# Second summands of weight halves added one half product sooner on VectorE, with their loads, in a two-layer mixer

## The chip, the cores and the metric

The kernel runs on one core of a Trainium2 chip. The metric is the device time of one execution in microseconds (us), median of the runs; lower is better. Engines are named as the profile names them: PE (TensorE matmul), DVE (VectorE), ACT (ScalarE), POOL (GpSimd), SP (SyncE, which here only issues loads).

## The reference

Two post-norm layers over a residual stream of 512 rows by 2048 columns. Each layer projects the stream once, runs three groups of heads, gates them, projects back and normalises:

```
h = einsum('bsd,dn->bsn', x, w_in)             # 2048 -> q, k, v, gates of 16 heads, index q/k/w
y_fox = fox_attention(...) * silu(fg)          # 6 heads, forget gate
y_dsa = dsa_attention(rope(dq), rope(dk), dv, q_idx, k_idx, w_idx) * silu(dg)   # 6 heads, top 128 of 512 keys
y_mem = memory_attention(mq, k_mem, v_mem) * silu(mg)                           # 4 heads, 256 memory rows
y = concat(y_fox, y_dsa, y_mem) @ w_out
x = layer_norm(ALPHA * x + y, ln_gain, ln_bias)
```

All is float32, and the result has to be that of float32 products. The top 128 keys of each query row come from an index score that all heads share.

## The kernel before

**Products.** A float32 product is made of three matmuls: each operand is split into a high part and the remainder (`split`: ACT writes `whi`, the high part; DVE writes `wlo`, the remainder, raw minus `whi`), and `product` sums hi\*hi, hi\*lo and lo\*hi. The large projections are also cut into 2x2 blocks and multiplied with seven products in place of eight (`PRODUCTS`: P1, P7, Q4, P2, Q6, Q5, Q3), some of whose right sides are sums of weight blocks.

**The stream.** `stream()` fixes a list of chunks of weights for both layers: memory values and keys, the index projection, then the *values* stage (`vs` chunks, all projections of values, gates and head inputs, six column pairs), the *heads* stage (Q5 and Q3 of the same projections, while the attention heads run) and the *out* stage. A chunk is 128 x 2048 floats and is used in two halves of 512 KB, h = 0 and 1. The main loop goes over halves, n = 2i + h. In the values stage a half is 12 matmuls of 128 x 512 columns on PE. For each column pair the chunks come in the order P1 0, P7 0, P1 1, P7 1, P2 0, Q6 0, Q6 1, P2 1, Q4 0, Q4 1 (the digit is the block of 1024 rows of weights), then one or two head chunks.

**Where right sides come from.** Most chunks are loaded as they are ("wall"). Sums for P7 of pair 0, for Q5 and for the out stage are made in DRAM by POOL, with accumulating transfers (tile `sum`), and then loaded. Q6 and Q4 are made on chip from raw halves that are done with (`make_w`, `raw<-raw,raw` on DVE). P7 of pairs 1 to 5 ("pair") is a sum of two weight blocks: `load_w` loads the first block's half into `raw` (SP, L373) and the second block's half as two tiles `other` of 128 x 512 (SP, L379), and `pair_w` adds the two on DVE, in two instructions `raw<-raw,other` of 128 x 512.

**What sets the order.** Each engine executes its instructions in the order in which the program emits them, and waits at each until its operands are there. In step n of the main loop the program emits, in this order: the loads of a chunk two ahead (`load_w`), `split_w(n + 3)` (ACT `whi`, DVE `wlo`, then `make_w` where that half gives a raw away), `pair_w(n + 4)`, the matmuls of half n, and, between them (`advance`, `tick`), pieces of the other work: the top-128 search (on DVE: `m<-acc` MAX, then `acc<-m,acc` MATCH_REPLACE), residual rows, copies of finished values. Raw halves live in seven buffers (`raws`), and a load waits for the last reader of the buffer's tenant before; `whi` and `wlo` have four buffers each. `other` tiles come from a shared pool of 69 slots, which values on their way to DRAM use as well. SP issues all loads of weights, of residual rows (`z<-x`, `row`) and of head inputs, in program order.

**Names for halves below.** In one column pair, m and m+1 are the halves of P7 0, m+2 and m+3 those of P1 1, m+4 and m+5 those of P7 1; m-2 and m-1 are those of P1 0. So m, m+1, m+4 and m+5 need a second summand.

Of the kernel before, what the change touches and what calls it, by code (L numbers as in the profile page):

```python
# [35 lines left out]
SCALE = HD ** -0.5  # L36
SOON, LATER, URGENT, DUE = 1.5, 4.0, 5.0, 10.0
SLOTS = 69
PACE = 2
R_ATTEND, R_QK, R_LOAD, R_MEM = 4, 5, 4, 8  # L40

# [216 lines left out]
def kernel(  # L258
# [13 lines left out]
    clock = Clock()  # L272
    nc = Engines(tc.nc, clock)
    consts = ctx.enter_context(tc.tile_pool(name="consts", bufs=1))
    raws = ctx.enter_context(tc.tile_pool(name="raws", bufs=7))
    whl = ctx.enter_context(tc.tile_pool(name="whl", bufs=4))
    slots = ctx.enter_context(tc.tile_pool(name="slots", bufs=SLOTS))
    tiny = ctx.enter_context(tc.tile_pool(name="tiny", bufs=3))
# [6 lines left out]
    def uid(name):  # L285
        count[0] += 1
        return f"{name}_{count[0]}"
# [43 lines left out]
    chunks = stream()  # L331
    raw, parts = {}, {}
# [46 lines left out]
                        nc.sync.dma_start(t, wall[key[1]][:, e * 512:(e + 1) * 512])  # L379

    others = {}

    def pair_w(n):

        i, h = divmod(n, 2)
        if i < len(chunks) and chunks[i][4][0] == "pair":
            for e in range(2):
                d = raw[i][h][:, e * 512:(e + 1) * 512]
                nc.vector.tensor_tensor(d, d, others.pop((i, 2 * h + e)), op=ALU.add)
# [160 lines left out]
    def block(kind, l, pair, g, step):  # L550
        return wall[where[kind, l, 2 * pair + step[1], 2 * step[0] + g]]

    def add_weights(key, src):
        nc.gpsimd.dma_start(sums[key], src, accum_op=ALU.add, max_dma_last_dim=2 * DM)

    def weight_sums(kind, l, names, pairs, some=(0, 1)):

        for name in names:
            for n in some:
                step = SUM_STEPS[name][n]  # L560
                for pair in pairs:
                    for g in range(2):
                        key = (kind, l, name, pair, g)
                        src = block(kind, l, pair, g, step)
                        pool_waits()
                        if n:
                            add_weights(key, src)
                        else:
                            sums[key] = dram.tile([P, DM], F32, name=uid("sum"))
                            nc.gpsimd.dma_start(sums[key], src, max_dma_last_dim=2 * DM)  # L570
                        yield

    def paced(gen):

        n = 0
        for _ in gen:
            n += 1
            while now[1] in ("kv", "heads"):
                yield 1
            yield {"out": 3, "index": 1 + n % 2}.get(now[1], PACE)  # L580

# [1020 lines left out]
    for i, (kind, l, j, col, _) in enumerate(chunks):  # L1602
        late = last_half(i)
        if kind == "out":
            step = OUT_ORDER.index(j)
            name, pair = j
# [3 lines left out]
            chain, aname, _, targets = PRODUCTS[name]  # L1610
# [9 lines left out]
        elif kind == "vs":  # L1620
            name, pair = j
# [13 lines left out]
        for h in range(2):  # L1635
            n = 2 * i + h
# [1 line left out]
            if n in late_makes:  # L1638
                make_w(late_makes[n])
            if i > 0:  # L1640
                late_half = i > 8 and i + 2 < len(chunks) and chunks[i + 2][4][0] != "pair"
                if late_half:
                    load_w(i + 2, 2, (h,))
                elif h == 0:
                    load_w(i + 2)
            if h == 0 and i > 0:
                if 2 <= i < 6:
                    for k in range(4 * i - 8, 4 * i - 4):
# [8 lines left out]
                splits[n + 3] = flow(split_steps(n + 3), 1e9, clock.at["PE"] + DUE)  # L1657
            else:
                split_w(n + 3)
            pair_w(n + 4)  # L1660
            for k in range(2 * n - 20, 2 * n - 18) if n < 16 else range(12, 16) if n == 16 else ():
                if k >= 0:
                    split_x(k)
# [43 lines left out]
            elif kind == "mk":  # L1707
                for kk in range(8):
                    k = 8 * h + kk
                    m = memT[k // 2]  # L1710
# [13 lines left out]
        if kind == "mk":  # L1724
            t = slot("kmem", F32R)
# [19 lines left out]
        elif kind == "small":  # L1745
# [4 lines left out]
            t = index_rope(ps, 64, 0, nc.vector)  # L1750
# [8 lines left out]
        elif kind == "iq":  # L1759
            t = index_rope(ps, P, P, nc.vector)  # L1760
# [137 lines left out]
```

## Time and profile before

| | |
|---|---|
| time, median of 3 runs (lowest to highest) | 1885.79 us (1884.57 to 1889.16) |
| profiled execution | 1885.75 us, span 1884.0 us |
| PE busy | 1854.5 us, 98% |
| DVE busy | 1606.9 us, 85% |
| ACT busy | 1079.0 us, 57% |
| POOL busy | 404.9 us, 21% |
| mean granted clock of TensorE | 0.997 of full |
| adds of second summands on DVE | 80, median 685 ns each |
| makes on DVE (`raw<-raw,raw`) | 88, median 1225 ns each |
| remainders on DVE (`wlo`) | 497, mean 1217 ns each |

Busy times are sums over one execution. A row of the timeline has its start (us from the span's start), its length, engine, line, operation, written tile, read tiles, shape and, in brackets, the engine's idle time before it with what ended that time. All compute instructions have line L242, a helper that records each of them; so groups are told apart by tile, not by line. A run of equal instructions stands as one row with a count (x2).

### The profile page before, as it was taken

Reading aid. Unit: us, or ns where it says so; the run is one execution under the profiler, and the core shown is the slowest. Engines: PE = TensorE matmul, PEld = TensorE weight load, DVE = VectorE, ACT = ScalarE, POOL = GpSimd, SP = SyncE. Lnnn points to the kernel's source line nnn. Section 1 sums busy time; section 2 is a strip of 40 time slices with the busy share of each in tenths; the row PEclk is TensorE's granted clock in tenths of the full one; section 3 lists DMA queues with packets and bytes.
Section 4 is the critical chain, followed back from the end, with each engine's and each line's share of the span. In section 5 each row is a group of like instructions: output and inputs, shape, how many; then the busy total and the mean of one; then the engine's idle time right before and its main releaser. Section 6 shows DMA issues by size and latency. Waiting matters only on the chain.

```text
span 1884.0 us, 26451 instructions
## 1 busy us (share of the span) xinstructions
PE 1854.5 (98%) x8994; PEld 1574.5 (84%) x8994; DVE 1606.9 (85%) x2565; ACT 1079.0 (57%) x1752; POOL 404.9 (21%) x595
## 2 busy tenths in 40 slices
PE   9999999999999999999999999999999999999997
PEld 8998888887888888888899977877878888888886
DVE  6789889888789987889887997898797898878798
ACT  5776344435347887555476653444354578875553
POOL 0121222122134311330011121221221343113302
PEclk9999999999999999999999999999999999999999
DMA  9885998898999978986598869988989998889866
GB/s 350 294 240 160 302 298 242 303 279 274 253 239 298 241 217 218 268 209 214 174 322 250 228 204 302 329 270 288 284 274 246 247 306 226 222 213 276 237 215 144
DMA packets 232165, 478.40 MB, mean 254 GB/s; under 512 B 76624, under 2 KB 101200, under 8 KB 231772
## 3 DMA queue, kind: packets, MB, share of 16 engines
q1 hardware_dynamic: 177660, 302.58, 49.8%
q0 software_dynamic: 53792, 173.06, 35.7%
q8 instruction: 71, 1.16, 0.2%
q10 hardware_dynamic: 576, 1.05, 0.1%
q14 instruction: 66, 0.54, 0.1%
HBM read 404.24 MB, written 152.07 MB: 295 GB/s over the span
## 4 chain that ended last, share of the span: by engine, by line
PE 70%; DVE 14%; DMA 8%; issue 4%; ACT 3%; SPq 0%; POOL 0%; DVEq 0%; ACTq 0%; POOLq 0%
PE v L242 30%; PE c L242 17%; PE z L242 15%; DVE wlo L242 6%; DMA other<-in_wall_dram 4%; DMA raw<-in_wall_dram 3%; PE po L242 3%; DVE raw L242 2%; PE s L242 2%; DVE acc L242 1%; ACT whi L242 1%; PE ix L242 1%; PE pt L242 1%; DMA v<-vraw 1%; DVE rope L242 1%
## 5 line engine op out<-in xcount | busy, mean ns | idle before, releaser
L242 ACT ACTIVATE whi<-raw 128x1024 fp32r<-128x1024 f32 (+1 forms) x497 | 521.2, 1056 | 473.5 <-PE v L242 190.9
L242 DVE TENSOR_TENSOR wlo<-raw,whi 128x1024 fp32r<-128x1024 f32 (+1 forms) x497 | 601.0, 1217 | 115.8 <-ACT whi L242 113.6
L242 PE MATMUL v<-whi,vxh 128*128 128x512 f32 x768 | 306.3, 399 | 6.8 <-ACT whi L242 3.2
L242 PE MATMUL v<-wlo,vxh 128*128 128x512 f32 x768 | 301.4, 392 | 7.9 <-DVE wlo L242 7.9
L242 PE MATMUL v<-whi,vxl 128*128 128x512 f32 x768 | 300.5, 391 | 0.0
L242 PE MATMUL v<-whi,xh 128*128 128x512 f32 x576 | 224.2, 389 | 0.0
L242 PE MATMUL v<-whi,xl 128*128 128x512 f32 x576 | 224.1, 389 | 0.0
L242 PE MATMUL v<-wlo,xh 128*128 128x512 f32 x576 | 224.1, 389 | 0.0
L242 PE MATMUL c<-xh,whi 128*128 128x512 f32 (+1 forms) x544 | 197.9, 364 | 0.0
L242 PE MATMUL c<-xh,wlo 128*128 128x512 f32 (+1 forms) x544 | 197.8, 364 | 0.0
L242 PE MATMUL c<-xl,whi 128*128 128x512 f32 (+1 forms) x544 | 197.7, 363 | 0.0
L242 POOL TENSOR_TENSOR seen<-mark,mhalf 128x1 f32<-128x1 f32 x88 | 48.3, 549 | 636.3 <-ACT mark L242 447.3
L242 PEld LDWEIGHTS v<-whi,vxh 128*128 128x128 f32 x768 | 144.7, 188 | 40.1 <-ACT whi L242 7.2
L242 PEld LDWEIGHTS v<-wlo,vxh 128*128 128x128 f32 x768 | 144.9, 189 | 39.3 <-DVE wlo L242 12.5
L242 PE MATMUL z<-wlo,yh 128*128 128x512 f32 (+1 forms) x434 | 167.8, 387 | 2.3 <-DVE wlo L242 2.3
L242 PEld LDWEIGHTS v<-whi,vxl 128*128 128x128 f32 x768 | 144.5, 188 | 30.4
L242 PE MATMUL z<-whi,yh 128*128 128x512 f32 (+1 forms) x434 | 168.6, 389 | 0.0
L242 PE MATMUL z<-whi,yl 128*128 128x512 f32 (+1 forms) x434 | 167.7, 387 | 0.0
L242 PEld LDWEIGHTS v<-wlo,xh 128*128 128x128 f32 x576 | 108.1, 188 | 22.6
L242 PEld LDWEIGHTS v<-whi,xh 128*128 128x128 f32 x576 | 108.1, 188 | 22.5
L242 PEld LDWEIGHTS v<-whi,xl 128*128 128x128 f32 x576 | 108.1, 188 | 22.5
L242 PEld LDWEIGHTS c<-xl,whi 128*128 128x128 f32 x544 | 102.1, 188 | 12.2
(209 smaller groups left out, 3459.9 us busy)
## 6 DMA issues: line engine op xcount, KB each, us to landing
raw<-in_wall_dram SPq DMA_DIRECT2D x331, 512.0 KB, 7.3
sum<-in_wall_dram POOLq DMA_DIRECT2D x88, 1024.0 KB, 10.4
raw<-sum SPq DMA_DIRECT2D x72, 512.0 KB, 7.4
v<-vraw POOLq DMA_DIRECT2D x88, 256.0 KB, 8.8
other<-in_wall_dram SPq DMA_DIRECT2D x80, 256.0 KB, 13.7
vt<-halves POOLq DMA_DIRECT2D x56, 256.0 KB, 9.4
vraw<-v SPq DMA_DIRECT2D x56, 256.0 KB, 5.1
grown<-in_wall_dram POOLq DMA_DIRECT2D x48, 256.0 KB, 8.9
```

The costliest lines, as they stand in the source:

```text
L242: return f(*args, **kw)
```

## The change

Three things are changed. `pair_w` is called with n + 5 instead of n + 4, so that the adds of a half's second summand come one split earlier in DVE's order. Loads go through `load_half`, which loads each half once; the halves of a "pair" chunk are loaded one step sooner than before (`soon`), to go with that. And `load_more` issues, in each step after chunk 8, up to two further halves, up to 14 halves ahead, as long as fewer than six of the seven raw buffers are in use, and only sums that POOL finished 20 us before by the planner's clock.

```diff
+RAWS, FAR, SETTLE = 7, 14, 20.0
...
+    loaded, settled = set(range(6)), {}
+
+    def load_half(m):
+        if m not in loaded:
+            loaded.add(m)
+            load_w(m // 2, 2, (m % 2,))
+
+    def raws_used():
+        return len({id(t) for v in raw.values() for t in v if t is not None and not isinstance(t, list)})
+
+    def load_more(n):
+
+        m = n + 4
+        for _ in range(2):
+            while m in loaded or (m < 2 * len(chunks) and chunks[m // 2][4][0] == "grown"):
+                m += 1
+            if m > n + FAR or m >= 2 * len(chunks) or raws_used() >= RAWS - 1:
+                return
+            kind, l, j, _, (how, key) = chunks[m // 2]
+            if kind == "out" and j[0] == "P7" or how == "pair" and len(others) > 2:
+                return
+            if how == "sum" and settled.get(key, 1e9) + SETTLE > clock.at["PE"]:
+                return
+            load_half(m)
...
                         if n:
                             add_weights(key, src)
+                            settled[key] = clock.at["PE"]
...
             if i > 0:
-                late_half = i > 8 and i + 2 < len(chunks) and chunks[i + 2][4][0] != "pair"
-                if late_half:
-                    load_w(i + 2, 2, (h,))
-                elif h == 0:
-                    load_w(i + 2)
+                soon = chunks[min((n + 5) // 2, len(chunks) - 1)][4][0] == "pair" or i <= 8 and h == 0
+                for m in (n + 4, n + 5) if soon else (n + 4,) if i > 8 else ():
+                    load_half(m)
...
-            pair_w(n + 4)
+            pair_w(n + 5)
+            if i > 8:
+                load_more(n)
```

The orders of PE, ACT and POOL stay as they were; DVE's and SP's move. The numbers behind a tile's name are buffers and differ between the two kernels; lines after the new functions shift by one, then by 27.

The first place is DVE at P7 0 of column pair 4 of layer 1. Before (`raw_13188` is half m, `raw_13194` half m+1, `raw_13146` and `raw_13164` the raws of P1 0, halves m-2 and m-1; `m<-acc` and `acc<-m,acc` are the top-128 search):

```order
L242 TENSOR_TENSOR wlo_13201<-raw_13164,whi_13200 128x1024
L242 TENSOR_TENSOR raw_13188<-raw_13188,other_13190 128x512
L242 TENSOR_TENSOR raw_13188<-raw_13188,other_13192 128x512
L242 MAX m_2827_13235<-acc_10251 128x8
L242 MATCH_REPLACE acc_10251<-m_2827_13235,acc_10251 128x512
L242 TENSOR_TENSOR wlo_13243<-raw_13188,whi_13242 128x1024
L242 TENSOR_TENSOR raw_13188<-raw_13188,raw_13146 128x1024
L242 TENSOR_TENSOR raw_13194<-raw_13194,other_13196 128x512
L242 TENSOR_TENSOR raw_13194<-raw_13194,other_13198 128x512
L242 MAX m_2833_13275<-acc_10251 128x8
L242 MATCH_REPLACE acc_10251<-m_2833_13275,acc_10251 128x512
L242 TENSOR_TENSOR wlo_13285<-raw_13194,whi_13284 128x1024
```

The same place in the changed kernel (`raw_13089` is half m, `raw_13118` half m+1, `raw_13038` and `raw_13067` the raws of P1 0; `vraw` are finished values leaving PSUM):

```order
L243 TENSOR_TENSOR raw_13089<-raw_13089,other_13093 128x512
L243 TENSOR_TENSOR vraw_12871<-vraw_12871,v_12800 128x512
L243 TENSOR_TENSOR vraw_12879<-vraw_12879,v_12801 128x512
L243 MAX m_2823_13202<-acc_10261 128x8
L243 MATCH_REPLACE acc_10261<-m_2823_13202,acc_10261 128x512
L243 TENSOR_TENSOR wlo_13207<-raw_13067,whi_13206 128x1024
L243 TENSOR_TENSOR raw_13118<-raw_13118,other_13120 128x512
L243 TENSOR_TENSOR raw_13118<-raw_13118,other_13122 128x512
L243 MAX m_2829_13241<-acc_10261 128x8
L243 MATCH_REPLACE acc_10261<-m_2829_13241,acc_10261 128x512
L243 TENSOR_TENSOR wlo_13249<-raw_13089,whi_13248 128x1024
L243 TENSOR_TENSOR raw_13089<-raw_13089,raw_13038 128x1024
```

The adds of m+1 stood behind `wlo` and the make of m; now they stand ahead of both, and the adds of m ahead of `wlo` of m-1 and of two reads of PSUM.

The second place is DVE at P7 1 of the same pair. Before (`raw_13330` is m+4, `raw_13336` m+5, `raw_13302` m+3):

```order
L242 TENSOR_TENSOR wlo_13343<-raw_13302,whi_13342 128x1024
L242 TENSOR_TENSOR raw_13330<-raw_13330,other_13332 128x512
L242 TENSOR_TENSOR raw_13330<-raw_13330,other_13334 128x512
L242 TENSOR_TENSOR wlo_13361<-raw_13330,whi_13360 128x1024
L242 TENSOR_TENSOR raw_13330<-raw_13330,raw_13282 128x1024
L242 TENSOR_TENSOR raw_13336<-raw_13336,other_13338 128x512
L242 TENSOR_TENSOR raw_13336<-raw_13336,other_13340 128x512
L242 MAX m_2857_13379<-acc_10251 128x8
L242 MATCH_REPLACE acc_10251<-m_2857_13379,acc_10251 128x512
L242 TENSOR_TENSOR wlo_13385<-raw_13336,whi_13384 128x1024
```

and in the changed kernel (`raw_13253` is m+4, `raw_13297` m+5, `raw_13142` and `raw_13168` are m+2 and m+3):

```order
L243 TENSOR_TENSOR wlo_13317<-raw_13142,whi_13316 128x1024
L243 TENSOR_TENSOR raw_13253<-raw_13253,other_13255 128x512
L243 TENSOR_TENSOR raw_13253<-raw_13253,other_13257 128x512
L243 MAX m_2850_13339<-acc_10261 128x8
L243 MATCH_REPLACE acc_10261<-m_2850_13339,acc_10261 128x512
L243 TENSOR_TENSOR wlo_13345<-raw_13168,whi_13344 128x1024
L243 TENSOR_TENSOR raw_13297<-raw_13297,other_13299 128x512
L243 TENSOR_TENSOR raw_13297<-raw_13297,other_13301 128x512
L243 TENSOR_TENSOR wlo_13363<-raw_13253,whi_13362 128x1024
L243 TENSOR_TENSOR raw_13253<-raw_13253,raw_13142 128x1024
L243 MAX m_2858_13381<-acc_10261 128x8
L243 MATCH_REPLACE acc_10261<-m_2858_13381,acc_10261 128x512
```

Between the adds of m+4 and the remainder of m+4 there now stand one search step, the remainder of m+3 and the adds of m+5.

The third place is SP ahead of P7 0 of column pair 2 of layer 1, where loads of residual rows (`z<-x`, `row`) share the queue. Before:

```order
L373 DMA raw_11872<-in_wall_dram 128x1024
L1455 DMA row_11985<-in_gain_dram 128x512
L1455 DMA row_11987<-in_bias_dram 128x512
L1519 DMA z_11989<-x_183 128x512
L373 DMA raw_11994<-in_wall_dram 128x1024
L373 DMA raw_12014<-in_wall_dram 128x1024
L373 DMA raw_12042<-in_wall_dram 128x1024
L373 DMA raw_12060<-in_wall_dram 128x1024
L373 DMA raw_12084<-in_wall_dram 128x1024
L379 DMA other_12086<-in_wall_dram 128x512
L379 DMA other_12088<-in_wall_dram 128x512
```

and in the changed kernel:

```order
L374 DMA raw_11879<-in_wall_dram 128x1024
L374 DMA raw_11902<-in_wall_dram 128x1024
L374 DMA raw_11920<-in_wall_dram 128x1024
L374 DMA raw_11953<-in_wall_dram 128x1024
L374 DMA raw_11975<-in_wall_dram 128x1024
L380 DMA other_11977<-in_wall_dram 128x512
L380 DMA other_11979<-in_wall_dram 128x512
L1482 DMA row_11999<-in_gain_dram 128x512
L1482 DMA row_12001<-in_bias_dram 128x512
L1546 DMA z_12003<-x_183 128x512
```

The raws and the first half's second summand (`raw_12084` before, `raw_11975` now, is half m) stood behind the residual row's loads and now stand ahead of them. At the start of layer 1's values stage and in both heads stages raws move ahead of residual rows and of head inputs in the same way; in layer 0's values stage and in pairs 4 and 5 of layer 1 SP's order of loads of weights and residual rows is as before; in pair 3 of layer 1 three loads of residual rows change places with one or two raws.

More of the change, by code (lines that the diff above doesn't have):

```diff
@@ L274 @@
     consts = ctx.enter_context(tc.tile_pool(name="consts", bufs=1))
-    raws = ctx.enter_context(tc.tile_pool(name="raws", bufs=7))
+    raws = ctx.enter_context(tc.tile_pool(name="raws", bufs=RAWS))
     whl = ctx.enter_context(tc.tile_pool(name="whl", bufs=4))
```

## Prediction, before the changed kernel was run

> **What bounds the kernel now.** The page first: which engine fills the span, and what DVE waits for.
>
> ```profile
> span 1884.0 us, 26451 instructions
> PE 1854.5 (98%) x8994; PEld 1574.5 (84%) x8994; DVE 1606.9 (85%) x2565; ACT 1079.0 (57%) x1752; POOL 404.9 (21%) x595
> ...
> L242 DVE TENSOR_TENSOR wlo<-raw,whi 128x1024 fp32r<-128x1024 f32 (+1 forms) x497 | 601.0, 1217 | 115.8 <-ACT whi L242 113.6
> ...
> other<-in_wall_dram SPq DMA_DIRECT2D x80, 256.0 KB, 13.7
> ```
>
> PE is busy for 1854.5 of 1884.0 us, so only some 30 us can be had from waits at all, start and end among them. The profiled execution took 1885.75 us, 1.75 more than its span and 0.04 less than the median, so a sum against it is a sum against the median. DVE's 113.6 us of waiting for ACT before a remainder look large, and an add next to its own remainder makes part of them: but idle time on DVE counts only where PE runs dry. So the second view is PE's busy time by stretches of the values stage (start to end, length, PE busy, granted clock, share of the DMA engines, GB/s).
>
> ```profile
> 425.00:480.00 55.00, 53.70 (x236) 1.00 0.85 278
> 1083.00:1130.00 47.00, 44.65 (x200) 1.00 0.69 203
> 1130.00:1180.00 50.00, 48.47 (x206) 0.97 0.92 305
> 1180.00:1240.00 60.00, 58.44 (x257) 1.00 0.97 312
> 1300.00:1346.00 46.00, 45.04 (x198) 1.00 0.81 239
> 1346.00:1378.00 32.00, 29.31 (x126) 1.00 0.90 270
> ```
>
> They leave 1.30, 2.35, 1.53, 1.56, 0.96 and 2.69 us idle, 10.4 in all: the ends of P7 in layer 0's pair 4 and layer 1's pairs 1 to 4, and the start of layer 1's values stage. Third, PE's own rows: where it stalls, and for whom.
>
> ```profile
> 1113.21 0.50 PE L242 MATMUL v<-wlo,vxh 128*128 128x512 f32 x1 [1.76 <-DVE wlo L242]
> ...
> 1164.61 0.39 PE L242 MATMUL v<-whi,vxl 128*128 128x512 f32 x1
> 1165.78 0.50 PE L242 MATMUL v<-whi,vxh 128*128 128x512 f32 x1 [0.78 <-ACT whi L242]
> 1167.04 0.59 PE L242 MATMUL v<-wlo,vxh 128*128 128x512 f32 x1 [0.76 <-DVE wlo L242]
> 1167.42 0.63 PE L242 MATMUL v<-whi,vxl 128*128 128x512 f32 x1
> 1167.85 0.63 PE L242 MATMUL v<-whi,vxh 128*128 128x512 f32 x1
> ...
> 1171.27 0.40 PE L242 MATMUL v<-whi,xh 128*128 128x512 f32 x1
> 1171.50 0.40 PE L242 MATMUL v<-wlo,xh 128*128 128x512 f32 x1
> ...
> 1358.55 0.50 PE L242 MATMUL v<-wlo,vxh 128*128 128x512 f32 x1 [0.83 <-DVE wlo L242]
> ...
> 1370.86 0.50 PE L242 MATMUL v<-whi,vxh 128*128 128x512 f32 x1 [0.90 <-ACT whi L242]
> 1372.16 0.50 PE L242 MATMUL v<-wlo,vxh 128*128 128x512 f32 x1 [0.80 <-DVE wlo L242]
> ```
>
> Undisturbed matmuls start 0.23 us apart (1171.27, 1171.50), 12 to a half, so a half lasts 2.72 us (estimate). From 1164.61 to 1165.78 and on to 1167.04 there are 1.17 and 1.26, so the two stalls lose 0.94 and 1.03, 2.0 together, somewhat more than the idle columns say. Behind them matmuls start 0.43 apart (1167.42, 1167.85). There the granted clock is low:
>
> ```profile
> 1164.00:1168.00 4.00, 2.46 (x9) 0.91 0.62 200
> 1168.00:1172.00 4.00, 4.00 (x14) 0.66 0.59 122
> ```
>
> The missing 0.09 and 0.34 of 4 us each are 1.7 us, which stand as busy time. So layer 1's pair 1 costs 3.7, not 2.0. With this, 10.4 + 1.7 and some 1.0 for what the idle columns hide, the values stage holds about 13 us; more the change can't gain there.
>
> Fourth, DVE in the worst pair (layer 1, pair 4), from m to m+5:
>
> ```profile
> 1347.85 1.23 DVE L242 TENSOR_TENSOR raw<-raw,raw 128x1024 f32<-128x1024 f32 x1
> ...
> 1355.28 0.69 DVE L242 TENSOR_TENSOR raw<-raw,other 128x512 f32<-128x512 f32 x1 [2.58 <-DMA other<-in_wall_dram]
> 1355.89 0.69 DVE L242 MAX8 m<-acc 128x8 f32<-128x512 f32 x1
> ...
> 1357.28 1.22 DVE L242 TENSOR_TENSOR wlo<-raw,whi 128x1024 fp32r<-128x1024 f32 x1
> ...
> 1365.89 1.23 DVE L242 TENSOR_TENSOR wlo<-raw,whi 128x1024 fp32r<-128x1024 f32 x1 [1.26 <-ACT whi L242]
> ...
> 1370.89 1.22 DVE L242 TENSOR_TENSOR wlo<-raw,whi 128x1024 fp32r<-128x1024 f32 x1
> ```
>
> Two waits are to be seen. At 1355.28 DVE waits for the second summand of m+1 to land; at 1365.89 it waits 1.26 for ACT's `whi`, because add and remainder of m+4 are neighbours. The tile's own view has the sums (what ended idle time before the adds, and before those that waited for the adds; us, times):
>
> ```profile
>   DMA other<-in_wall_dram: 33.1, 20
> ...
>   ACT whi L242: 107.7, 28
> ```
>
> The neighbours' wait is what the change removes. The landing is older and is the cause here: from 1355.28 to 1370.89 DVE idles only for that 1.26, and PE waits for its last remainder. After a late second summand DVE's work bounds PE.
>
> **The change, part by part.**
>
> *Late pairs whose summands land when they did.* After the last late add, DVE's order before held five remainders, two makes, two double adds and three search steps until m+5 is split; 15.6 us from 1355.28 to 1370.89, the 1.26 idle included. In the new order the remainder of m and its make stand behind that add too, and one more search step: 1.22 + 1.23 + 1.39 (1355.89 to 1357.28) = 3.84, of which starts overlap by some 0.1 each, so 3.6. The idle 1.26 goes, since a search step and another half's work lie between. Net +2.4, say +2.5. From the other side: if DVE runs under a PE that has enough split halves, it costs nothing. Layer 1's pair 4 is behind already (2.69 us idle): +2.5. Layer 0's pair 4 and layer 1's pair 3 have stalls at the end of P7 (1.30 and 0.96 idle): +2 each, as part of it meets what is left of slack. Layer 0's pair 1 shows no stall at P7: +1, between 0 and 2.5. Sum +7.5, bounds 0 and +10.
>
> *The remainder of m now waits for m+1's summand.* In pair 4 it would start at 1357.3, where the one of m+1 stood, and end near 1358.5. On PE m+1 began near 1358.5 after a stall of about 1.1, so m, 2.72 earlier and without that stall, is due near 1354.7: PE would stand some 3.8 us in one place. This is not added: it is the same lateness, moved forward, and the end is still set by DVE's chain.
>
> *Buffers.* The raw of m+5 takes the buffer that the make of m frees:
>
> ```profile
> 1349.14 0.33 SPq L373 DMA_DIRECT2D raw<-in_wall_dram  x1
> ...
> DMA to landing us min/median/max: 14.4/14.4/14.4
> ...
> DMA to landing us min/median/max: 4.7/4.7/4.7
> ```
>
> It was issued at 1349.14, as the make (1347.85 + 1.23) ended, and took 14.4 us among the others; one issued near 427.5 with little around it took 4.7. The make now ends behind the add at 1355.28: + 0.69 + 1.39 + 1.22 + 1.23 = 1359.8, so this load starts 10.7 later. Its add is due about 1368.5: 1359.8 and, in the new order, a search step (1.39), a remainder, a make and a remainder (1.15 each from start to start), the adds of m+4 (1.3), a search step (1.39) and a remainder (1.2). Landing at 1364.5 (4.7) it is hidden; at 1374.2 (14.4), with its second summand some 1.5 behind, the pair loses 7. By then the queue is nearly empty, as the other loads of the pair were issued before, so I take the value near 4.7: +0.4 for each of four late pairs, +1.5; bounds 0 and +28.
>
> *Loads ahead in layer 1.* In pair 2 SP stood still in front of a residual row:
>
> ```profile
> 1180.63 0.33 SPq L1455 DMA_DIRECT2D row<-in_bias_dram  x1
> 1188.64 0.33 SPq L1519 DMA_DIRECT2D z<-x  x1
> 1189.07 3.93 SPq L373 DMA_DIRECT2D raw<-in_wall_dram  x5
> 1196.77 2.28 SPq L379 DMA_DIRECT2D other<-in_wall_dram  x2
> ```
>
> Five raws came 8 us late and then together, and the second summand behind them. With the raws ahead of `row` and `z` that goes, and the second summand leaves about 4 us sooner (half of the 8, as it waits for transfers in flight as well). That covers the +2.5 of the longer chain and the present 1.56: -1.5, between 0 and -2. In pair 1 it leaves sooner in the same way (an estimate from the same rows): the stalls of 2.0 go, and likely the low clock behind them: -3, between 0 and -3.7. At the stage's start:
>
> ```profile
> 1084.72 2.24 ACT L242 ACTIVATE whi<-raw 128x1024 fp32r<-128x1024 f32 x2 [1.55 <-DMA raw<-in_wall_dram]
> ```
>
> ACT waits there for raws that now leave some 10 us sooner; the 2.35 us of the first window hang on this partly, and partly on the operands of the left side: -1.5, between 0 and -2.4.
>
> *Heads and out.* Here raws and sums go ahead of head inputs, which then leave up to some 14 us later (estimate from SP's order and the times before). The tightest of them shows:
>
> ```profile
> POOL bt L242 <- DMA ck<-crow: 21.8, 4, 8.4
> ```
>
> POOL already waits for `ck` up to 8.4 us at four heads while PE goes on with the products; POOL is busy for 21% of the span. I cost this at 0; with that cover gone, +4 (half of the 8.4 once more, in one layer).
>
> Sum: 7.5 + 1.5 - 1.5 - 3 - 1.5 = +3.0, and 1885.75 + 3.0 = 1888.8, rounded to **1889 us**.
>
> **Rivals.** *The neighbours' wait is the bound* (faster). For it: each stall at m+5 is a wait for `whi`, then `wlo`, right behind an add (1165.78, 1370.86), and the change takes just these apart; second summands may also land sooner in every pair. Against it: the chain from 1355.28 has no other slack, and gets longer. Then most of the 13 us go: 1873 to 1878, say 1876.
>
> *The freed buffer decides* (slower). The raw of m+5 leaves 10.7 us later, takes nearer 14.4 than 4.7, and the remainder of m+4, which now stands behind the add of m+5, waits too. It decides from a landing of more than 9 us on. Then four late pairs lose 3 to 7 more than the chain: about 1889 + 12 = 1901. Against it: the emptier queue.
>
> *Head inputs behind the raws* (slower): +4 and the +3, 1893.
>
> *Crowding* (slower). The DMA engines are busy for 0.92 and 0.97 of pairs 1 and 2 of layer 1 (windows above). Raws sent ahead then only change places with the second summands in flight, the three gains fall to their bounds of 0, and 1885.75 + 9.0 is 1895. Against it: the 8 us in which SP issued nothing. The Trainium skill ("DMA: Bandwidth & Descriptors", Issuing engines are not separate DMA queues) speaks for it: transfers of all issuing engines share the same DMA engines and interleave. The shares agree with that.
>
> *The gate* (slower). PE's stall of 3.8 us in the two pairs 4 and a like one in layer 1's pair 3 let the clock fall as at 1167: 1.7 us in each, if PE and not DVE then sets the end: 1889 + 5 = 1894. Against it: behind such a stall DVE is later than PE. By the Trainium skill ("TensorE: Matmul & The Clock Gate", HAM oscillation) an idle gap of more than about 3.4 us closes the gate; this trace differs, since two gaps of about 1 us closed it at 1167 and two like them at 1370 did not.
>
> *Nothing*: the waits move and the work under PE takes up both, 1886.
>
> **How the numbers follow.** What a measurement of this kernel can tell from no change is about 0.3%, 5.7 us: faster is below 1880, slower above 1891.5. The forecast has 0.40 (0.03 faster, 0.27 same, 0.10 slower, its terms as uncertain as their bounds), the neighbours 0.25 (0.22 faster, 0.03 same), the buffer 0.17 (0.15 slower, 0.02 same), heads 0.05 (0.02 slower, 0.03 same), crowding 0.04 (slower), the gate 0.04 (0.03 slower, 0.01 same), nothing 0.05 (same). Faster 0.25, same 0.41, slower 0.34. The range takes in the forecast, the gate, crowding, the heads, nearly half of the buffer's case and the upper third of the neighbours'; its lower end is the sum of all lower bounds (0 + 0 - 2 - 3.7 - 2.4 = -8.1): 1877 to 1898. The forecast's own is 1884 to 1893.
>
> **What would show it.** Right: in the late pairs DVE has no idle time between an add and its remainder, the remainder of m starts 10 us later than the make of m ended before, the stalls sit at m and m+1 and not at m+5 alone; in layer 1's pairs 1 and 2 the second summands are issued earlier, and no clock below 1.00 near 1167. The neighbours are right if PE's idle time in those windows nears zero; the buffer, if the add of m+5 waits for its own landing; the heads, if PE stalls after 1500. The forecast is wrong if the second summands land at other times in layer 0, where the same waits precede them.

## The result: 1.5% slower

The changed kernel takes 1912.70 us (median of five executions) against 1886.16 us before (median of six); the ratio is 1.0149, 95% interval 1.0127 to 1.0172. A sixth execution of the changed kernel took 2304.41 us at a granted clock of 0.752, where the others had 0.991 to 0.996, and is not counted. The prediction said 1889 us, range 1877 to 1898. The profiled execution of the changed kernel took 1910.05 us, so what follows accounts for 24 of the 27 us. The page, in its first part and its groups:

```profile
span 1908.2 us, 26460 instructions
PE 1861.2 (98%) x8994; PEld 1576.7 (83%) x8994; DVE 1606.6 (84%) x2565; ACT 1083.3 (57%) x1752; POOL 399.2 (21%) x595
...
L243 DVE TENSOR_TENSOR wlo<-raw,whi 128x1024 fp32r<-128x1024 f32 (+1 forms) x497 | 600.8, 1216 | 103.9 <-ACT whi L243 102.3
```

DVE's work is what it was (1606.6 against 1606.9), and its wait for ACT ahead of remainders, which the change aims at, fell from 113.6 to 102.3 us. What came in its place is in the tile's own view:

```profile
  DMA other<-in_wall_dram: 73.5, 38
...
  ACT whi L243: 84.2, 20
```

DVE now idles 73.5 us in 38 adds for a second summand to land; before, it was 33.1 in 20. PE's busy time by stretches that answer to those shown of before (the first is shorter, and pair 3 of layer 1 is left out; start to end, length, PE busy, granted clock, share of the DMA engines, GB/s), the last one in the heads:

```profile
412.00:440.00 28.00, 24.14 (x97) 0.94 0.82 252
1094.00:1141.00 47.00, 45.23 (x202) 1.00 0.65 189
1141.00:1192.00 51.00, 49.15 (x216) 1.00 0.93 301
1192.00:1256.00 64.00, 57.79 (x240) 0.95 0.93 284
1358.00:1402.00 44.00, 39.61 (x162) 0.92 0.85 247
570.00:640.00 70.00, 65.16 (x335) 1.00 0.97 261
```

The first, fourth and fifth leave 3.9, 6.2 and 4.4 us idle, with the clock below 1.00, and the heads 4.8. PE's longest stalls:

```profile
420.06 0.50 PE L243 MATMUL v<-wlo,vxh 128*128 128x512 f32 x1 [2.57 <-DVE wlo L243]
...
623.52 0.50 PE L243 MATMUL v<-whi,vxh 128*128 128x512 f32 x1 [3.44 <-DVE vraw L243]
...
1232.65 0.62 PE L243 MATMUL v<-wlo,vxh 128*128 128x512 f32 x1 [3.16 <-DVE wlo L243]
1248.46 0.50 PE L243 MATMUL v<-wlo,vxh 128*128 128x512 f32 x1 [3.05 <-DVE wlo L243]
...
1377.49 0.80 PE L243 MATMUL v<-wlo,vxh 128*128 128x512 f32 x1 [4.36 <-DVE wlo L243]
...
1578.66 0.50 PE L243 MATMUL v<-whi,vxh 128*128 128x512 f32 x1 [2.76 <-DVE vraw L243]
```

Behind four of these (420, 1232, 1248, 1377) the granted clock is low, in windows of 4 us; behind the two in the heads (623, 1578) it stays at 1.00, which the row at 624 shows for the first:

```profile
420.00:424.00 4.00, 3.94 (x10) 0.57 0.70 235
...
624.00:628.00 4.00, 4.00 (x23) 1.00 1.05 370
...
1232.00:1236.00 4.00, 3.35 (x8) 0.61 0.96 315
...
1248.00:1252.00 4.00, 3.54 (x11) 0.74 0.25 82
1252.00:1256.00 4.00, 4.00 (x16) 0.83 0.67 185
...
1376.00:1380.00 4.00, 2.51 (x6) 0.53 0.50 191
1380.00:1384.00 4.00, 4.00 (x12) 0.62 1.00 254
```

PE's order is the same in both kernels and all 8994 matmuls are recorded in both, so each matmul's start can be set against its own start before. The table has how much later PE got in each stretch, for the changed kernel and for the experiments that the next section explains (us of one profiled execution each; "L0 P4" is column pair 4 of layer 0's values stage; "rest" is what lies between).

| | L0 P1 | L0 P4 | L0 heads | L1 start | L1 P1 | L1 P2 | L1 P3 | L1 P4 | L1 heads | rest | all |
|---|---|---|---|---|---|---|---|---|---|---|---|
| the change | 1.8 | 4.6 | 4.9 | -0.6 | -1.2 | 7.8 | 1.5 | 3.8 | 3.4 | -1.8 | 24.2 |
| e1 adds alone | 2.0 | 3.1 | 0 | 0.6 | 0.9 | 6.6 | 0.6 | 3.4 | -0.1 | 0.3 | 17.4 |
| e9 first block's adds | 4.9 | 4.9 | 0 | -0.5 | 2.0 | 4.0 | 2.2 | 2.3 | 0.2 | 3.3 | 23.3 |
| e8 second block's adds | 0.1 | 1.4 | -0.2 | -0.3 | -1.0 | 0.7 | -0.4 | -1.9 | -0.1 | -0.4 | -2.1 |
| e7 adds, eight raws | 0 | 2.7 | 0 | -0.6 | -0.1 | 6.4 | 0 | 1.6 | 0.2 | 1.3 | 11.5 |
| e6 adds, one other | 0 | -1.9 | -0.2 | 0.2 | -3.8 | -2.1 | -1.6 | -3.0 | -0.1 | 0.2 | -12.3 |
| e10 before, eight raws | 0 | 0.4 | 0 | -0.6 | -0.2 | 6.0 | -1.5 | -3.0 | -0.1 | 1.0 | 2.0 |
| e2 loads alone | 0 | -0.1 | 5.7 | -0.6 | -2.6 | 3.0 | -0.8 | -0.5 | 6.5 | -0.5 | 10.1 |
| e13 loads in values | -0.1 | 2.1 | 0.9 | -0.6 | -3.0 | 3.1 | -0.9 | 1.4 | 0.8 | 1.5 | 5.2 |
| e14 loads in heads | 0.1 | 1.0 | 1.8 | 1.0 | -1.9 | 1.5 | -0.5 | -0.5 | 5.2 | -1.6 | 6.1 |
| e4 rows behind pair | 1.3 | 3.0 | 3.2 | -0.6 | -0.8 | 7.5 | 0.8 | 1.4 | 5.9 | -1.1 | 20.6 |

Stretches also differ where two kernels have the same order. The change and e4 have different orders in a few loads of layer 1's pair 2 alone, and yet they are 1.6 us apart in layer 0's pair 4, and some 2.4 us in layer 1's pair 4 and, the other way, in layer 1's heads. So single entries under some 2.5 us say little.

So the loss has two places: some 18 us in the values stages, at P7 of pairs whose second summands land late, and 8 us in the heads, less some 2 elsewhere. Pairs 2, 3 and 5 of layer 0 and 5 of layer 1 lose nothing.

**At P7.** DVE in layer 1's pair 4, the pair that the prediction worked out, in the changed kernel:

```profile
1363.11 0.69 DVE L243 TENSOR_TENSOR raw<-raw,other 128x512 f32<-128x512 f32 x1 [2.42 <-DMA other<-in_wall_dram]
...
1370.94 0.69 DVE L243 TENSOR_TENSOR raw<-raw,other 128x512 f32<-128x512 f32 x1 [3.42 <-DMA other<-in_wall_dram]
1374.21 0.69 DVE L243 TENSOR_TENSOR raw<-raw,other 128x512 f32<-128x512 f32 x1 [2.58 <-DMA other<-in_wall_dram]
...
1376.22 1.22 DVE L243 TENSOR_TENSOR wlo<-raw,whi 128x1024 fp32r<-128x1024 f32 x1
1377.46 1.22 DVE L243 TENSOR_TENSOR raw<-raw,raw 128x1024 f32<-128x1024 f32 x1
...
1388.34 0.69 DVE L243 TENSOR_TENSOR raw<-raw,other 128x512 f32<-128x512 f32 x1 [0.40 <-DMA other<-in_wall_dram]
1388.95 1.22 DVE L243 TENSOR_TENSOR wlo<-raw,whi 128x1024 fp32r<-128x1024 f32 x1
...
1392.74 1.22 DVE L243 TENSOR_TENSOR wlo<-raw,whi 128x1024 fp32r<-128x1024 f32 x1
```

The remainder at 1376.22 is that of m. Its own sum was ready at 1363.8 (the adds of m ended there, 1363.11 + 0.69), but it stands behind the adds of m+1, for which DVE waits 3.42 and 2.58 us. PE stands 4.36 us. The neighbours' idle time is gone (1388.34, 1388.95), yet from the last late add to the remainder of m+5 it is 18.53 us (1374.21 to 1392.74), before 15.6: the 1.26 saved is less than the remainder, the make and the search step that moved behind the landing (3.6 us by the prediction's rows). With the summand 0.8 later beside PE's course than before (18.93 later in time, PE 18.1), that is 3.7 of this pair's 3.8.

In layer 1's pair 2 the loss is greatest. DVE there:

```profile
1216.71 1.22 DVE L243 TENSOR_TENSOR wlo<-raw,whi 128x1024 fp32r<-128x1024 f32 x1
1227.87 1.41 DVE L243 TENSOR_TENSOR raw<-raw,other 128x512 f32<-128x512 f32 x2 [9.95 <-DMA other<-in_wall_dram]
1229.19 1.41 DVE L243 TENSOR_TENSOR z<-z,row 128x512 f32<-128x512 f32 x2
...
1250.91 1.22 DVE L243 TENSOR_TENSOR wlo<-raw,whi 128x1024 fp32r<-128x1024 f32 x1
```

and SP's queue ahead of it:

```profile
1203.52 1.03 SPq L380 DMA_DIRECT2D other<-in_wall_dram  x2
1204.65 0.47 SPq L1482 DMA_DIRECT2D row<-in_gain_dram  x1
1206.98 0.33 SPq L1482 DMA_DIRECT2D row<-in_bias_dram  x1
1208.07 0.33 SPq L1546 DMA_DIRECT2D z<-x  x1
...
1209.53 0.99 SPq L380 DMA_DIRECT2D other<-in_wall_dram  x2
```

The second summand of m left at 1203.52, ahead of the loads of `row` and `z`, but that of m+1 only behind them, at 1209.53. DVE idles 9.95 us for it, with the remainder of m ready to be made behind it, and then adds the residual rows (1229.19) ahead of that remainder as well. The kernel before has, for the last add of m+1 and the remainder of m+5:

```profile
1219.17 0.69 DVE L242 TENSOR_TENSOR raw<-raw,other 128x512 f32<-128x512 f32 x1 [2.22 <-DMA other<-in_wall_dram]
...
1234.86 1.23 DVE L242 TENSOR_TENSOR wlo<-raw,whi 128x1024 fp32r<-128x1024 f32 x1
```

The last add of m+1 now starts at 1228.59 (the second of the two at 1227.87), 9.4 us later, where PE runs 8.9 us later: beside PE's course that is only 0.6. What grew is the chain behind it, from 15.7 us to 22.3 (1228.59 to 1250.91). And e1, which sends no load ahead, loses 6.6 us in this pair as well, so most of the 7.8 comes with the adds.

**In the heads.** ACT now waits for head inputs, for which it had no wait before. Between 530 and 700 us (groups of waits: total, times, longest):

```profile
ACT qh L243 <- DMA vraw<-vt: 5.9, 2, 3.0
...
ACT vh L243 <- DMA vraw<-v: 2.3, 2, 1.4
```

Two of them in ACT's timeline:

```profile
614.05 0.64 ACT L243 ACTIVATE qh<-vraw 128x512 fp32r<-128x512 f32 x1 [2.88 <-DMA vraw<-vt]
...
618.12 0.63 ACT L243 ACTIVATE vh<-vraw 128x512 fp32r<-128x512 f32 x1 [1.44 <-DMA vraw<-v]
```

Behind these in ACT's order stands a `whi`; on DVE its remainder waits for it, and behind the remainder stands the `vraw<-vraw,v` that empties a PSUM bank:

```profile
620.66 1.59 DVE L243 TENSOR_TENSOR wlo<-raw,whi 128x1024 fp32r<-128x1024 f32 x1 [2.86 <-ACT whi L243]
...
622.79 0.68 DVE L243 TENSOR_TENSOR vraw<-vraw,v 128x512 f32<-128x512 f32 x1
```

For that bank PE waits 3.44 us at 623.52. At 588.82 it is shorter: ACT's `vraw`, which empties a bank there, stands behind 0.93 us of waiting for `vraw<-vt` and 0.81 for `vraw<-v`, and PE waits 1.40 us.

### The profile page after: what moved, and what is told of

Read it like the earlier page. It is cut to its first block, busy times and chain, and to the rows that moved or that the text cites. A ratio compares the mean times of both kernels' runs of the same rounds, so it can differ in the third digit from the quotient of the medians.

```text
span 1908.2 us, 26460 instructions
## 1 busy us (share of the span) xinstructions
PE 1861.2 (98%) x8994; PEld 1576.7 (83%) x8994; DVE 1606.6 (84%) x2565; ACT 1083.3 (57%) x1752; POOL 399.2 (21%) x595
## 5 line engine op out<-in xcount | busy, mean ns | idle before, releaser
L243 DVE TENSOR_TENSOR wlo<-raw,whi 128x1024 fp32r<-128x1024 f32 (+1 forms) x497 | 600.8, 1216 | 103.9 <-ACT whi L243 102.3
L243 DVE TENSOR_TENSOR raw<-raw,other 128x512 f32<-128x512 f32 x80 | 53.6, 688 | 73.5 <-DMA other<-in_wall_dram 73.5
```

What stands on the lines that cost most here:

```text
L243: return f(*args, **kw)
```

## The experiments

Theories. *Order*: an add that stands ahead of the remainder and make of the half before holds DVE up whenever its summand is late, and that is the loss in the values stages. *Queue*: the loads that were sent ahead delay others on SP or crowd them, and that is the loss. *Buffer*: part of it comes from the raw of m+5, whose buffer the make of m frees. All ratios are against the kernel before on the same chip, with 95% intervals.

### Adds alone, loads alone

e1 leaves out `load_more`:

```diff
             pair_w(n + 5)
-            if i > 8:
-                load_more(n)
```

> The change without load_more: VectorE's order is that of the changed kernel, SP's is that of the kernel before but for two residual loads. Order theory (the adds, now ahead of the remainder and the make of the half before, hold VectorE up when a second summand lands late): most of the loss in the values stage stays, some 6.7 us in layer 0 (its loads never moved) and 8 to 10 in layer 1's pairs 1 to 4, none in the heads: about 1.008 times before, 1901 us. Queue theory (the loads sent ahead crowd or delay others): layer 0's 6.7 at most, heads and layer 1 as before: 1.000 to 1.0035, 1886 to 1893.

Measured: 1.0085 (1.0066 to 1.0103), 1904.99 us. e2 keeps the loads and puts the adds back:

```diff
-            pair_w(n + 5)
+            pair_w(n + 4)
```

> The changed loads with the adds at their old place: SP's order is that of the changed kernel, VectorE's that of the kernel before. Order theory: layer 0's values as before, layer 1's pair 2 loses 1 to 3 as the second summand of m+1 still comes late, heads lose the 6.8 us that they lose now, the start of layer 1's values wins 1: about 1.004, 1893 us. Queue theory: nearly all of the loss stays, 1.010 to 1.015, 1905 to 1915 us.

Measured: 1.0046 (1.0031 to 1.0061), 1895.68 us. Both are what the order theory said, 16 and 8.7 us; they add up to 1.0131, inside the interval of the whole. By the table, e1 has its loss in the values stages alone and e2 in the heads, with a gain in layer 1's pair 1 and a loss in its pair 2.

### Is it the late landing that makes the order cost?

e5 (kernel before) and e6 (e1) load the second summand of m alone and use it for the pair's other three halves (`shared` hands out the tiles of m). The sums that they compute are therefore others:

```diff
-                if kind == "pair":
-                    for e in (2 * c, 2 * c + 1):
+                if kind == "pair" and c == 0 and chunks[i][3] == 0:
+                    for e in (0, 1):
...
-                nc.vector.tensor_tensor(d, d, others.pop((i, 2 * h + e)), op=ALU.add)
+                nc.vector.tensor_tensor(d, d, shared(i, h, e), op=ALU.add)
```

> The kernel before, with one second summand loaded per column pair in place of four: the adds of m+1, m+4 and m+5 use the tiles of m, and six of the eight 256 KB loads of a pair are left out (another sum, so the result isn't the reference's). It has the neighbours' wait as before, but fewer late landings. Order theory: VectorE's wait for second summands (33.1 us before) falls under 8, and PE's stalls at P7 with it: 0.994 to 0.997, 1877 to 1882 us. If the neighbours' wait bounds the pairs, the stalls at m+5 stay and the time is that of before, 0.998 to 1.000.

> The same leaving out of six of eight loads of second summands, in the kernel with the adds alone sooner (no load_more). Order theory: an add that finds its summand landed holds nothing up, so the loss of 16 us falls to under 4 against the kernel before with the same loads left out: 0.995 to 0.999. If the order costs by itself (more work between a landing and the last remainder, whatever lands when), the loss stays: 1.005 to 1.008.

Measured: e5 0.9935 (0.9912 to 0.9959), e6 0.9947 (0.9926 to 0.9967). With most summands there in time the order costs 0.0012, some 2 us and within the intervals, where it costs 16 with all loads. The tile's view, e5 then e6:

```profile
  DMA other<-in_wall_dram: 8.2, 6
...
  ACT whi L242: 86.5, 26
```

```profile
  DMA other<-in_wall_dram: 22.1, 10
...
  ACT whi L243: 23.0, 10
```

In e5 the neighbours' wait is mostly there (86.5 us of ACT waiting for adds, 107.7 before), and still 12 us are won: the neighbours did not bound the pairs, the late landings did. In e6 it is 23.0, and nothing more is won. (Leaving out loads also frees the DMA engines for the others, so these runs show the late landing as a whole, not one transfer.)

### Which adds?

e9 moves the adds of m and m+1 alone, e8 those of m+4 and m+5 alone; both are e1 with

```diff
-            pair_w(n + 5)
+            for m, g in ((n + 4, 1), (n + 5, 0)):   # e9; e8 has ((n + 4, 0), (n + 5, 1))
+                if m < 2 * len(chunks) and chunks[m // 2][3] == g:
+                    pair_w(m)
```

> The counterpart: the adds of m and m+1 alone one split sooner, those of m+4 and m+5 at their old place, no load_more. Order theory: these are the adds whose summands land late, so the whole loss of the adds alone stays, with the neighbours' wait on top: 1.007 to 1.010, 1900 to 1906 us. If the loss needs both blocks' adds to move: under 1.004.

> The adds of m+4 and m+5 alone one split sooner, those of m and m+1 at their old place, no load_more; loads as in the kernel before but for two residual loads. Before, the summands of m+4 and m+5 were always there (no wait in the trace), so order theory says that nothing is held up there and only the neighbours' 1.26 us go, twice in each late pair: 0.997 to 0.9995, 1880 to 1885 us. If moving any add sooner costs, as the longer chain would have it: 1.002 to 1.005.

Measured: e9 1.0099 (1.0084 to 1.0115), e8 0.9994 (0.9982 to 1.0005). The first block's adds carry the whole loss; the second block's, moved alone, cost nothing and win nothing that can be told from nothing. They were not free of waits, as had been expected: in e8 DVE waits 14.7 us for the summands of m+4 and m+5 in 15 adds, none of them over 3.3 us, where it waited 0.4 us in one before. These short waits cost nothing, and moving these adds, with the neighbours' wait partly gone (77.9 us of ACT waiting for adds), is worth at most 3.4 us (0.0018 of 1887).

### The buffer

e7 is e1 with eight raw buffers and two slots fewer; e10 is the kernel before with the same, as control.

```diff
-RAWS, FAR, SETTLE = 7, 14, 20.0
+RAWS, FAR, SETTLE = 8, 14, 20.0
...
-SLOTS = 69
+SLOTS = 67
```

> The kernel with the adds alone sooner, with eight raw buffers in place of seven and 67 slots in place of 69, so that the raw of m+5 takes a buffer that is free long before the make of m. Buffer theory: VectorE's waits before the adds of m+5 (0.9, 2.0, 4.1 and 0.7 us in layer 0's pairs 1 and 4 and layer 1's pairs 2 and 4) vanish, and 4 to 8 of the 16 us with them: about 1.005, 1897 us. If the wait for m+1 is all, nothing changes: 1.0085.

> The kernel before with eight raw buffers and 67 slots: the control of the run with eight buffers. Before, no add of m+5 waited for its summand, so by the buffer theory an eighth buffer has nothing to give: 0.998 to 1.001. If it gives 0.997 or less, part of what it gave with the adds sooner is not the freed buffer of the make.

Measured: e7 1.0062 (1.0043 to 1.0082), e10 1.0021 (1.0010 to 1.0031). The control is slower itself, beyond what was expected, with 6.0 us lost in layer 1's pair 2; which of the two sizes does that was not tried. Against its control the adds cost 0.0041, some 8 us, where they cost 16 with seven buffers; the intervals leave 3 to 14 us for the difference. That is the size which the theory asked for, but not by its way. The eighth buffer does free the load: in layer 1's pair 4 the raw of m+5 leaves at 1352.98 in e7, 11 us ahead of the end of m's make (1364.13), where in e1 it leaves as that make ends (1374.13 and 1374.07). Yet DVE's waits before the adds of m+5 do not vanish. They are 13.8 us in 9 adds in e7, where e1 has 8.3 in 7 (7.7 of them in the four pairs named). One of e7, in layer 1's pair 2:

```profile
1238.06 0.69 DVE L243 TENSOR_TENSOR raw<-raw,other 128x512 f32<-128x512 f32 x1 [3.74 <-DMA other<-in_wall_dram]
```

The second summands of m+5 that leave sooner take longer: in pair 4 18.7 and 16.8 us in e7, 5.3 and 8.9 in e1. What fell in e7 are the waits at m and m+1, from 60.2 us to 35.4. So that the buffer's release costs half of the order's loss is not shown; how e7 gets its time back stays open. In the changed kernel that raw leaves at 1378.75 in layer 1's pair 4, as the make of m (from 1377.46) ends, and lands 4.4 us later; its second summands take longer than the raw. DVE in layer 1's pair 2 of the changed kernel, at the adds of m+5:

```profile
1244.39 0.69 DVE L243 TENSOR_TENSOR raw<-raw,other 128x512 f32<-128x512 f32 x1 [2.21 <-DMA other<-in_wall_dram]
1246.57 0.69 DVE L243 TENSOR_TENSOR raw<-raw,other 128x512 f32<-128x512 f32 x1 [1.49 <-DMA other<-in_wall_dram]
```

These 3.70 us are more than half of the 6.6 by which DVE's chain from the last late add to the remainder of m+5 grew in layer 1's pair 2.

### The loads sent ahead

e3 is the change with `load_more` in the values stages alone; e13 the same with the adds at their old place; e14 has `load_more` in the heads alone, adds at their old place.

```diff
-            if i > 8:
+            if i > 8 and now[1] == "values":        # e14: "heads"
                 load_more(n)
```

> The change with load_more in the values stages alone, so that heads and out load as before (but for five raws at the start of each heads stage). If head inputs late on SP cost the heads' stalls (588.8, 623.5, 1578.7 in the profile after), 6.8 us come back: about 7 us under the changed kernel, and the heads' stalls are those of before. If these stalls are the values' lateness carried on, nothing comes back.

> load_more in the values stages alone, all adds at their old place: the loads of the changed kernel without those in the heads. The prediction put layer 1's values 6 us better by such loads and the heads at 0. If that gain is real and only hidden by the adds: 0.997 to 0.999. If loads sent ahead there only change places with later ones: 0.999 to 1.002.

> load_more in the heads stages alone, all adds at their old place. If the heads' head inputs, queued behind raws on SP, are what the loads cost (stalls of 4.3 and 2.5 us in the changed kernel's heads): 1.003 to 1.006, 1892 to 1898 us. If the stalls came from the values' lateness: 0.999 to 1.001.

Measured: e3 1.0110 (1.0089 to 1.0131), 7 us under the change, as expected, but with intervals that overlap. Its one profiled execution is no shorter than the change's: the values stages lose more, and of the heads only layer 1's come back (0.8 us lost), while layer 0's still lose 3.9, with a stall of 2.14 us at 590.28. So e3 alone doesn't show what the heads' loads cost. e13 1.0025 (1.0013 to 1.0037), slower than both theories had it; e14 1.0036 (1.0021 to 1.0051). In e14 the heads' stalls are there without any lateness from the values:

```profile
615.18 0.50 PE L243 MATMUL v<-whi,vxh 128*128 128x512 f32 x1 [2.40 <-DVE vraw L243]
...
1558.97 0.50 PE L243 MATMUL v<-whi,vxh 128*128 128x512 f32 x1 [4.15 <-DVE vraw L243]
```

So the heads lose 7 us by their own loads (1.8 and 5.2); in layer 0 the parts don't add up, as e2 with all loads loses 5.7 there. In e13 layer 1's pair 1 gains 3.0, its pair 2 loses 3.1 again, and the rest is spread (five raws still go ahead at the start of each heads stage); what makes its 4.7 us in all is not settled. The ratios of e1, e13 and e14 add up to 1.0146, inside the interval of the whole.

e4 puts the three residual loads of layer 1's pair 2 behind the loads of m+1:

```diff
             load_half(m)
+            if how == "pair" and m % 2 == 0:
+                load_half(m + 1)
```

> The change with both halves of a pair chunk sent together by load_more, which moves only the loads of two rows and one residual tile in layer 1's pair 2 from between the loads of m and m+1 to behind them. If these three loads make the second summands of m+1 late there (they left at 1209.5 and landed at 1228, before at 1200 and 1219), pair 2's loss of 6.7 us falls to about 2, and the time to some 5 us under the changed kernel. If the late landing comes from crowding, nothing changes.

Measured: 1.0098 (1.0080 to 1.0117), 10 us under the change, but not by the expected way: pair 2 loses 7.5 us, where it lost 7.8. What makes the 10 us is not known, as all other orders are those of the change; so differences of that size between two such runs need care, e3's 7 us too. The summands of m+1 are now in time (adds at 1214.9 and 1215.5 without a wait), and the next instruction in DVE's order takes the wait, in DVE's timeline of e4:

```profile
1225.80 1.42 DVE L243 TENSOR_TENSOR z<-z,row 128x512 f32<-128x512 f32 x2 [9.61 <-DMA z<-x]
```

The residual tile lands at 1225.7, and the remainder of m stands behind it. In both orders tried the load that goes last in that burst holds up an instruction ahead of the remainder.

### Loads earlier for all

e11: the adds at their old place, eight raw buffers, 67 slots, and every load after chunk 8 one half product sooner; e12: the same with the adds of m+4 and m+5 one split sooner.

```diff
-                for m in (n + 4, n + 5) if soon else (n + 4,) if i > 8 else ():
+                for m in (n + 4, n + 5) if i <= 8 and h == 0 else () if i <= 8 else (n + 4, n + 5, n + 6) if soon else (n + 4, n + 5):
```

> The adds at their old place, eight raw buffers, 67 slots, and all loads after chunk 8 issued one half product sooner (no load_more). If late landing of second summands is what is left to win (5 to 7 us less with six of eight loads left out), issuing them 2.7 us sooner takes part of it: 0.996 to 0.999, 1878 to 1884 us. If the DMA engines are full there, loads sent sooner land no sooner: 0.999 to 1.002.

> The same with the adds of m+4 and m+5 one split sooner. Both small wins add if both theories hold: 0.994 to 0.998, 1875 to 1883 us; with full DMA engines the time of the second block's adds alone, 0.999 to 1.001.

Measured: e11 0.9990 (0.9977 to 1.0002), e12 1.0020 (1.0010 to 1.0030). In e11 DVE's wait for second summands falls to 22.3 us in 16 adds, 33.1 before, and against its own control (e10, 1.0021) that is worth 0.003; against the kernel before it is no difference. e12 is slower than e11, against the expectation; why the second block's adds cost there what they did not cost in e8 stays open. No version tried beats the kernel before beyond its interval with all work done.

## Why the prediction was wrong

*What bounds the pairs: right.* "After a late second summand DVE's work bounds PE" held, and its size too: with six of eight loads of second summands left out the kernel before gets 12 us faster, where the prediction put about 13 us into the values stage. The neighbours' wait was rightly not taken as the bound (e5, e8).

*Late pairs: mechanism right, size too small.* Predicted +7.5 for layer 0's pairs 1 and 4 and layer 1's 3 and 4, and +1.5 for their buffers; the profile has 1.8 + 4.6 + 1.5 + 3.8 = 11.7. In pair 4 of layer 1 the chain grew by 2.9 (2.4 worked out), PE's gap was 4.36 (3.8), and beside PE's course (18.1 later) the remainder of m came 9 us behind the end of the make before (10). In layer 0's pair 4 the prediction's +2 was 4.6: the wait at the add of m+5 is 1.1 of it, and the summand of m+1 landed 2.45 later (its add at 416.79, before 414.34) where PE ran only 1.4 later.

*"This is not added: it is the same lateness, moved forward": right where it can be read.* Behind PE's stall at m the pair's end is still set by DVE's chain. In layer 0's pair 4 PE stops again for the remainder of m+5 (0.77 us at 437.29), and in layer 1's pair 4 that remainder ends at 1393.96 and its first matmul starts at 1394.02. What the step had too small is what stands in the chain: in layer 1's pair 2 it grew by 6.6 us, not by the 2.5 that each late pair was given, 3.70 of it waits for the second summands of m+5, and the adds of the residual rows (1.4 us) moved behind the landing as well. DVE's idle time is no price by itself: it stands 73.5 us for summands in place of 33.1, as it comes to those adds earlier.

*Buffers: mis-sized.* Predicted +1.5, bounds 0 and +28. The price of a raw alone was right (4.4 landing against 4.7 taken), but two second summands follow it in the queue, and they were later: 8.3 us of waits before the adds of m+5 in e1, 6.9 in the changed kernel, where before there were none. How much of this is due to the buffer stays open, as such waits are there with eight buffers too (e7).

*Layer 1's loads ahead: the first step that failed; -6 was predicted, +6.0 measured.* For pair 2 the prediction gave -1.5 and the run has +7.8. It failed at "with the raws ahead of `row` and `z` that goes, and the second summand leaves about 4 us sooner": the order of SP, shown ahead of the prediction, has only half m ahead of them, and the loads of m+1, on which the remainder of m now waits, follow behind `row`, `row` and `z`. Their summand came 0.6 us later beside PE's course, not 4 sooner, so nothing covered the longer chain, and that chain cost 6.6 where 2.5 was counted. By e1 (6.6) most of the loss is the adds'; the loads alone lose 3.0 there (e2). And e4 shows that even with the loads of m+1 ahead something else in the burst lands last. Pair 1 gained 1.2 for -3. With the adds at their old place e13 gains 3.0 there, but e14, which sends nothing ahead in the values stages, gains 1.9, so the loads' own part is not clear. The start of the stage gained 0.6, not 1.5, and the kernel before gains as much there with eight buffers (e10).

*Heads: "I cost this at 0": wrong, +8.3.* This is the other step that failed. The prediction looked at `ck` and POOL, which has time, and took their wait for the tightest. That wait did grow, from 21.8 us (longest 8.4) to 38.9 (longest 17.4), but the waits ahead of PE's stalls came on ACT, for `vraw<-vt` and `vraw<-v`, which ACT had never waited for, so that no row of before showed them; and ACT's order has the next `whi` and DVE's has the emptying of a PSUM bank behind them. The price named for lost cover, +4 in one layer, is near that of each of the two stages (4.9 and 3.4), but by luck, as it was half of POOL's wait.

*The rivals.* The gate had a chance of 0.04, and it closed in three pairs, behind four stalls: the six rows of low clock above lose 4 x (0.43 + 0.39 + 0.26 + 0.17 + 0.47 + 0.38) = 8.4 us, 1.7 before. Little of it sets the end. In both pairs 4 the remainder of m+5 comes last, as said; in layer 1's pair 2 it ends at 1252.13 and PE uses it at 1252.50, so at most some 0.7 us there are the clock's. In e6, with most summands in time, no 4 us stretch ahead of 1860 has a clock under 0.98. The gaps ahead of the four are 2.57, 3.16, 3.05 and 4.36 us; gaps of 3.44 (623.52) and 2.76 (1578.66) left the clock at 1.00. The Trainium skill ("TensorE: Matmul & The Clock Gate", HAM oscillation) puts the limit at gaps of more than about 3.4 us; 2.57 closed it here and 3.44 did not. Heads had 0.05 with +4. Crowding had 0.04 and said that the three gains fall to 0; one of them turned into the largest loss, and what the transfers in flight have to do with it was not taken apart. The range left out that chain, heads and pair 2 all go against the change at once; each had been given its mild value.

## What to carry to other kernels

On an engine that executes in order, moving an instruction that waits for a transfer ahead of work that is ready makes everything behind it as late as that transfer: remove a small wait only where the moved instruction's data is there, or where its wait stays short, as the second block's did (none over 3.3 us in e8). When loads are sent ahead on a shared queue, list for every load that falls back its first reader, what stands behind that reader on its engine, and who needs that; a reader that never waited shows no row. And a buffer's release is an instruction like any other: if it moves behind a wait, the next load in that buffer waits as well.

## What the runs showed of the hardware

In the changed kernel TensorE's granted clock fell to 0.53 to 0.74 over 4 us behind single gaps of 2.57, 3.05, 3.16 and 4.36 us and stayed at 1.00 behind gaps of 3.44 and 2.76 us; before, it fell behind two gaps of 0.78 and 0.76 us that stood 1.3 us apart. A gap of 1.76 us at the start of layer 1's values stage left it at 1.00 before (at 1113.21) and was followed by 0.57 from 1116 to 1120 in e14 (at 1114.92). So in these runs the length of a gap alone does not say whether the clock falls. One half's raw and its two second summands, sent behind one another, did not land together: the raw landed 4.0 us after its issue at 421.3 and the last summand 9.4 us after its own at 422.2. In flight beside them were two second summands of m+1 until 423.6, a 1 MB sum that POOL issued at 421.26, and from 425.1 on the next raws.
